# Second layer of a two-layer encoder: values and gates by seven products of halves, with tokens on partitions

## The chip, the cores and the metric

One core of a Trainium2 chip runs the kernel. The metric is the device time of one launch in microseconds (us), taken as the median of several runs. A profile is one further execution, recorded instruction by instruction. The engines are PE (TensorE, the matrix products), DVE (VectorE), ACT (ScalarE), POOL (GpSimd) and SP (SyncE, which here only issues transfers).

## What is computed

The input is `x` of 512 tokens by 1024 channels in float32. Layer 0 mixes latent attention with a pooling mixer. Layer 1, the one that changes, is a bidirectional retention with 4 heads (256 channels for queries and keys, 512 for values). A final RMSNorm follows. Cut to layer 1:

```python
def retention_layer(x, ...):
    h = rms_norm(x, norm_g)
    q, k, v, gate = split(h @ w_in)          # w_in 1024 x 6144: q 1024, k 1024, v 2048, gate 2048
    q, k = rope(q), rope(k) * 256 ** -0.5
    o = forward + backward chunkwise retention(q, k, v)   # equals ((q k^T) * decay matrix) v
    o = (o - mean(o)) * rsqrt(var(o) + 1e-6)              # per head, over its 512 channels
    y = o * gn_g * silu(gate)
    return y @ w_out                         # w_out 2048 x 1024
```

The result is `rms_norm(x + layer 1)`.

## The kernel before

Every product is made in three matmuls (`mm3`, L72, L75, L76): each operand is cut into a rounded half H and the rest L, and H·H, H·L and L·H are added in one PSUM bank. Each matmul has a 128x128 stationary operand and 512 moving columns. A weight tile of 128 x 1024 is loaded by SP into a slot `raw` (3 slots), cast by ACT into `wH` (L108, 4 slots), and DVE subtracts to get `wL` (L109, 3 slots). A weight tile feeds 24 matmuls.

The code is written for one instruction after another, but a list scheduler orders each engine's queue: it takes the work in program order as priority and moves later work ahead where its operands and slots are free by its own cost model. Each engine then runs its queue strictly in that order; a waiting instruction holds all behind it. PSUM has 4 banks `mm`, 2 `sc` and 2 `tr`.

Layer 1 begins in `close_layer` (L651 to L657), which adds the last product of layer 0 to the residual `xT` (channels on partitions), scales it by the norm's gain and splits it into the 8 pairs `h2H`, `h2L`. The norm's factor per token is not multiplied in: it comes from `token_sums` (squares, then two matmuls with ones, L181 and L182), is spread by `bcast` (two matmuls, L209 and L210) into `R`, and multiplies what comes out. `acc_in` transposes the residual to tokens on partitions (L676).

For each head the loop at L828 runs: q and k (`qk_gemm`, 4 column tiles of 24 matmuls), `rope_pair`, the output projection of the head before (`r_out`, 96 matmuls), the decay matrix (`decay`), values (`r_values`, 4 weight tiles, 96 matmuls, tokens on partitions), scores (`r_scores`, 24 matmuls), gates (`r_gates`, 4 weight tiles, 96 matmuls, channels on partitions) and `r_head_out` (48 matmuls, channels on partitions). The group norm's factor needs a sum over channels, so each head has its `token_sums`; with those of the input norm that is five calls, and one `bcast`. After the last head come the projections of heads 2 and 3, and `finish` and `scale_out` make the last norm.

Of the kernel before, what the change touches and what calls it, by code (L numbers as in the profile page):

```python
# [19 lines left out]
P = 128  # L20
# [17 lines left out]
def trunk(ctx: ExitStack, tc: tile.TileContext, x, positions, a_norm_g, a_w_in, a_q_norm_g, a_w_uq,  # L38
# [84 lines left out]
    lg = C("lg", (P, 8))  # L123
    nlb = C("nlb", (P, 8))
    fsum = C("fsum", (P, 16))
    C("fill", (P, 40))
# [518 lines left out]

    h2H, h2L = [None] * 8, [None] * 8
    sqs = S("l1")
# [8 lines left out]
    w_out_quarter(3, ys2, close_layer)  # L658

    def decay(h):  # L660
        e = gp.rearrange("p a b -> p (a b)")[:, :E]
# [2 lines left out]
        act(e, e, AF.Exp)  # L664
        return [e[:, (3 - j) * P:(3 - j) * P + T] for j in range(4)]


    wr = r_w_in[0]
    wo = r_w_out[0]
    acc = [[None] * 2 for _ in range(4)]  # L670

    def acc_in(hf):
# [12 lines left out]
    def qk_gemm(c0, n=2):  # L685
        pts = []
        gemm_T(wr, c0, n, lambda m, pt: pts.append(pt), h2H, h2L)
        return pts

    def rope_pair(pts):  # L690
# [7 lines left out]
        return split(a, "qk"), split(c, "qk")  # L698

    def r_values(h):  # L700
        pts = [PS("mm") for _ in range(4)]
        for kp in range(4):
            uH, uL = wunit(wr[kp * 256:(kp + 1) * 256, 2048 + h * T:2048 + (h + 1) * T]
                           .rearrange("(k p) n -> p k n", p=P), 2, T)
            for k2 in range(2):
                k = kp * 2 + k2
                for t in range(4):
                    tk = slice(t * P, (t + 1) * P)
                    mm3(pts[t], h2H[k][:, tk], h2L[k][:, tk], uH[:, k2], uL[:, k2], k == 0, k == 7)
        vH, vL = [], []  # L710
        for t in range(4):
            v = S("t")
            sm = S("sm", (P, 4))
            act(v, pts[t], AF.Copy, scale=r2[:, t:t + 1], accum_out=sm[:, 0:1])
# [3 lines left out]
            act(hh, v, AF.Identity, bias=sm[:, 1:2])  # L718
            V.scalar_tensor_tensor(out=ll, in0=v, scalar=sm[:, 1:2], in1=f(hh), op0=ALU.add, op1=ALU.subtract)
            vH.append(hh)  # L720
            vL.append(ll)
        return vH, vL

    def r_scores(q, k, ds):
        sH, sL = [], []
        for j in range(4):
            tk = slice(j * P, (j + 1) * P)
            pt = PS("sc")
            for i in range(2):
                mm3(pt, k[i][0][:, tk], k[i][1][:, tk], q[i][0], q[i][1], i == 0, i == 1)  # L730
            s = S("t")
            V.scalar_tensor_tensor(out=s, in0=pt, scalar=0.0625, in1=ds[j], op0=ALU.mult, op1=ALU.mult)
            a, b = split(s, "pt")
            sH.append(a)
            sL.append(b)
        return sH, sL

    def r_gates(h, m0=0, n=4):
        gs = []

        def ev(m, pt):
            t = S("t")
            V.tensor_mul(t, pt, R)  # L743
            g = S("l1")
            act(g, t, AF.Silu)
            gs.append(g)

        gemm_T(wr, 4096 + h * T + m0 * P, n, ev, h2H, h2L)
        return gs

    def r_head_out(h, vv, ss, gs, ytag):
        ys = []
        sq = None
        for m in range(4):
            ms = slice(m * P, (m + 1) * P)
            pt = PS("mm")
            for j in range(4):
                mm3(pt, vv[0][j][:, ms], vv[1][j][:, ms], ss[0][j], ss[1][j], j == 0, j == 3)
            t = S("t")
            act(t, pt, AF.Square)  # L760
            if sq is None:
                sq = t
            else:
                V.tensor_add(sq, sq, t)
            y = S("t")
            V.scalar_tensor_tensor(out=y, in0=pt, scalar=col(GN + h * 4 + m), in1=gs[m], op0=ALU.mult, op1=ALU.mult)
            ys.append(split(y, ytag))
        return ys, sq

    def r_out(h, ys, rs, last=False, mid=None):  # L770
        for hf in range(2):
            us = [wunit(wo[h * T + i * 256:h * T + (i + 1) * 256, hf * T:(hf + 1) * T]
                        .rearrange("(k p) n -> p k n", p=P), 2, T) for i in range(2)]
            for t in range(4):
                tk = slice(t * P, (t + 1) * P)
                n = 2 if last and hf == 1 and t == 3 else 1
                for c in range(n):
                    cs = slice(c * T // n, (c + 1) * T // n)
                    pt = PS("mm")
                    for k in range(4):  # L780
                        mm3(pt[:, :T // n], ys[k][0][:, tk], ys[k][1][:, tk], us[k // 2][0][:, k % 2, cs],
                            us[k // 2][1][:, k % 2, cs], k == 0, k == 3)
# [43 lines left out]

    pend = None
    for h in range(4):  # L828
        if h == 0:
            pts = acc_in(0)  # L830
            pq = qk_gemm(0, 1)
            act(sqs, xT[0], AF.Square)
            for m in range(1, 8):
                t = S("t")
                act(t, xT[m], AF.Square)
                V.tensor_add(sqs, sqs, t)
            acc_set(0, pts)
# [3 lines left out]
            rp = bcast(r2)
            nc.scalar.copy(R, rp)
            V.tensor_mul(cosr, cosr, R)
            V.tensor_mul(sinr, sinr, R)
        else:
            pq = qk_gemm(h * 256)
            pk = qk_gemm(1024 + h * 256, 1)
            pend.append(pow_mhalf(token_sums(psq), 1.0 / T))
        q = rope_pair(pq)
        k = rope_pair(pk + qk_gemm(1024 + h * 256 + P, 1))  # L850
        if h == 0:
            acc_set(1, acc_in(1))
        if pend is not None and h < 3:
            r_out(*pend)
        ds = decay(h)
        if h == 0:
            gs = r_gates(h, 0, 2)
        vv = r_values(h)
        ss = r_scores(q, k, ds)
        gs = gs + r_gates(h, 2, 2) if h == 0 else r_gates(h)  # L860
        ys, sq = r_head_out(h, vv, ss, gs, "y" if h < 3 else "hT")
        if h == 3:
            for i in range(2):
                gt = S("l1")
                nc.scalar.dma_start(gt, final_norm_g[i * T:(i + 1) * T].partition_broadcast(P))
                gF.append(gt)
            own = []
            r_out(*pend, mid=lambda: own.append(pow_mhalf(token_sums(sq), 1.0 / T)))
            r_out(h, ys, own[0], last=True)
# [44 lines left out]
```

## Time and profile before

| | us |
|---|---|
| median of 3 runs | 807.08 (806.32 to 807.74) |
| the profiled execution | 807.98 |
| its span, first to last instruction | 806.2 |
| PE busy in the span | 796.5 (99%), 3590 matmuls |
| DVE busy | 524.1 (65%) |
| ACT busy | 364.4 (45%) |
| POOL busy | 18.9 (2%) |

A busy share counts an engine as busy while any of its instructions is in flight. Matmuls overlap, so one lasts about 390 ns while the next starts 227 ns later; the step from start to start is what a matmul costs.

### The profile page before, as it was taken

How to read it: one execution, taken by the hardware profiler on the slowest of the kernel's cores; microseconds unless marked ns; L12 is line 12 of the kernel's file. 1: busy time of each engine (PE TensorE's matmuls, PEld its weight loads, DVE VectorE, ACT ScalarE, POOL GpSimd, SP SyncE). 2: the span in 40 equal slices, each digit the busy share in tenths (PEclk: the TensorE clock that was granted, in tenths of full speed). 3: DMA queues.
4: the chain of work that ended last, by engine and by line, in shares of the span. 5: the costliest groups of instructions: out<-in, count | busy, mean ns of one | idle time of the engine just before them, and what ended most of it. 6: DMA issues, size and time to landing. Idle time of an engine off the chain costs nothing.

```text
span 806.2 us, 9481 instructions
## 1 busy us (share of the span) xinstructions
PE 796.5 (99%) x3590; PEld 656.1 (81%) x3590; DVE 524.1 (65%) x895; ACT 364.4 (45%) x595; POOL 18.9 (2%) x45
## 2 busy tenths in 40 slices
PE   8999999999999999999999999999999999999996
PEld 6888888888888888888888888888888888888885
DVE  4689976767748687899564648363483535753655
ACT  6645346676627734328254522263232543253222
POOL 0010000000000000000000000000000000000003
PEclk9999999999999999999999999999999999999999
DMA  7523233221222212233323113323123221232112
GB/s 224 150 75 90 85 82 75 54 80 62 72 81 80 79 53 78 79 101 111 103 79 105 52 53 105 98 59 105 53 68 115 79 78 53 85 99 78 53 53 104
DMA packets 93589, 68.30 MB, mean 85 GB/s; under 512 B 7484, under 2 KB 83304, under 8 KB 93544
## 3 DMA queue, kind: packets, MB, share of 16 engines
q1 hardware_dynamic: 93240, 67.18, 28.4%
q8 instruction: 28, 0.46, 0.3%
q10 hardware_dynamic: 304, 0.53, 0.2%
q14 instruction: 17, 0.14, 0.1%
HBM read 64.29 MB, written 2.10 MB: 82 GB/s over the span
## 4 chain that ended last, share of the span: by engine, by line
PE 97%; DMA 1%; POOL 1%; issue 0%; SPq 0%; ACT 0%; DVE 0%; POOLq 0%
PE mm L72 29%; PE mm L75 29%; PE mm L76 29%; PE sc L72 2%; PE sc L76 2%; PE sc L75 2%; PE tr L560 2%; PE sc L541 1%; PE sc L542 1%; DMA l<-in_x_dram 1%; POOL t L820 0%; POOL sm L816 0%; PE tr L182 0%; PE mm L345 0%; PE mm L344 0%
## 5 line engine op out<-in xcount | busy, mean ns | idle before, releaser
L108 ACT CAST wH<-raw 128x1024 fp32r<-128x1024 f32 (+3 forms) x133 | 125.4, 946 | 291.2 <-PE mm L75 137.4
L109 DVE TENSOR_TENSOR wL<-raw,wH 128x1024 fp32r<-128x1024 f32 (+3 forms) x133 | 144.5, 1090 | 94.5 <-PE mm L76 42.1
L72 PE MATMUL mm<-hT,wH 128*128 128x512 f32 x480 | 187.9, 391 | 0.0
L75 PE MATMUL mm<-hT,wH 128*128 128x512 f32 x480 | 187.6, 391 | 0.0
L76 PE MATMUL mm<-hT,wL 128*128 128x512 f32 x480 | 187.6, 391 | 0.0
L76 PEld LDWEIGHTS mm<-hT,wL 128*128 128x128 f32 x480 | 90.6, 189 | 18.9
L75 PEld LDWEIGHTS mm<-hT,wH 128*128 128x128 f32 x480 | 90.4, 188 | 18.7
L72 PEld LDWEIGHTS mm<-hT,wH 128*128 128x128 f32 x480 | 90.5, 189 | 18.5
L75 PE MATMUL mm<-wL,hT 128*128 128x512 f32 (+1 forms) x164 | 63.0, 384 | 0.0
L72 PE MATMUL mm<-wH,hT 128*128 128x512 f32 (+1 forms) x164 | 62.9, 384 | 0.0
L76 PE MATMUL mm<-wH,hT 128*128 128x512 f32 (+1 forms) x164 | 62.8, 384 | 0.0
L786 DVE SCALAR_TENSOR_TENSOR xT<-mm,sm,xT 128x512 f32<-128x512 f32 (+1 forms) x33 | 24.2, 732 | 23.8 <-PE mm L76 23.8
L743 DVE TENSOR_TENSOR t<-mm,R 128x512 f32<-128x512 f32 x16 | 11.1, 691 | 43.2 <-PE mm L76 43.2
L75 PE MATMUL mm<-pt,V 128*128 128x512 f32 x96 | 37.8, 393 | 0.0
L72 PE MATMUL mm<-pt,V 128*128 128x512 f32 x96 | 37.5, 391 | 0.0
L76 PE MATMUL mm<-pt,V 128*128 128x512 f32 x96 | 37.5, 390 | 0.0
L75 PE MATMUL mm<-wL,y 128*128 128x512 f32 x96 | 37.4, 389 | 0.0
L72 PE MATMUL mm<-wH,y 128*128 128x512 f32 x96 | 37.4, 389 | 0.0
L76 PE MATMUL mm<-wH,y 128*128 128x512 f32 x96 | 37.3, 389 | 0.0
L75 PE MATMUL mm<-y,wH 128*128 128x512 f32 x96 | 37.2, 389 | 0.0
L76 PE MATMUL mm<-y,wL 128*128 128x512 f32 x96 | 37.2, 389 | 0.0
L72 PE MATMUL mm<-y,wH 128*128 128x512 f32 x96 | 37.2, 390 | 0.0
(238 smaller groups left out, 1329.8 us busy)
## 6 DMA issues: line engine op xcount, KB each, us to landing
raw<-in_r_w_in_dram SPq DMA_DIRECT2D x48, 512.0 KB, 3.8
raw<-in_a_w_in_dram SPq DMA_DIRECT2D x25, 512.0 KB, 3.9
raw<-in_a_w_out_dram SPq DMA_DIRECT2D x16, 512.0 KB, 3.5
raw<-in_r_w_out_dram SPq DMA_DIRECT2D x16, 512.0 KB, 3.4
l<-in_x_dram SPq DMA_DIRECT2D x8, 256.0 KB, 5.6
out_dram<-t SPq DMA_DIRECT2D x8, 256.0 KB, 2.0
raw<-in_a_w_in_dram SPq DMA_DIRECT2D x4, 384.0 KB, 4.1
raw<-in_a_w_uq_dram SPq DMA_DIRECT2D x8, 192.0 KB, 2.4
```

The source lines that it names most:

```text
L72: i = mm(pt, lhsT=lH, rhs=rH, start=st, stop=False)
L75: mm(pt, lhsT=lH, rhs=rL, start=False, stop=False)
L76: mm(pt, lhsT=lL, rhs=rH, start=False, stop=sp)
L108: then(nc.scalar.copy(h[:, c], raw[:, c]))
L109: then(V.tensor_sub(l[:, c], raw[:, c], f(h[:, c])))
L541: mm(pt, lhsT=st[:, tk], rhs=KH, start=False, stop=False)
L542: mm(pt, lhsT=st[:, tk], rhs=KL, start=False, stop=True)
L560: nc.tensor.transpose(pt[:, t * P:(t + 1) * P], es[t][:, j * P:(j + 1) * P], ident)
L743: V.tensor_mul(t, pt, R)
L786: V.scalar_tensor_tensor(out=a, in0=pt[:, :T // n], scalar=rs[:, t:t + 1], in1=a, op0=ALU.mult, op1=ALU.add)
```

## The change

1. Values and gates of a head are the two halves of a 1024-column block of `w_in`, the tokens are two halves of 256 (`H2`), and the input channels are taken as even and odd blocks of 128. That makes a 2x2 by 2x2 block product, which the new function `vg` computes with seven block products where eight are usual. Each takes 24 matmuls and two weight tiles of its own. Values and gates both come out with tokens on partitions.
2. The seven products need sums of blocks of the activations (`sums_of_halves`, once, in head 0) and sums of blocks of the weights: for two of them (`tt` at its start, and `t3`) a second transfer adds into the landed tile (`G.dma_start(..., accum_op=ALU.add)`, four per head, issued by POOL); for the others DVE adds.
3. `r_head_out` makes outputs with tokens on partitions: the group norm's sum is then an ACT accumulation and `token_sums` goes away; the gated output is transposed on PE (16 transposes of 128x128 per head). The gain `gn_g` moves into the output weights (`out_weights`).
4. The input norm's sums are ACT accumulations on the residual with tokens on partitions (`residual`), and its factor is a per-partition scale (`r2`, `nr2`, `r2s`).
5. Scores are made before `vg`; `r_out` of head 2 runs in head 3's turn. `raw` has 4 slots instead of 3; `tw` (2 slots) holds weight sums.

```diff
@@ close_layer
-        h2H[m], h2L[m] = h, l
+        hH[m], hL[m] = h, l
+        for i, name in enumerate((("A11", "A21"), ("A12", "A22"))[m % 2]):
+            forms[m // 2][name] = (h[:, i * H2:(i + 1) * H2], l[:, i * H2:(i + 1) * H2])
+    def sums_of_halves(i):
+        e, o = S("t"), S("t")
+        for z, m in ((e, 2 * i), (o, 2 * i + 1)):
+            act(z, xT[m], AF.Copy, scale=col(RN + m))
+        z3, z4 = S("t"), S("t")
...
+        V.tensor_sub(z3[:, one], o[:, two], e[:, two])
+        V.tensor_sub(z4[:, one], e[:, one], e[:, two])
...
+            nc.scalar.copy(h, z)
+            V.tensor_sub(l, z, f(h))
...
@@ vg, in place of r_values and r_gates
+        tags = dict(X=("mm", "mm"), Z=("mm", "tr"), Y=("mm", "sc"))
...
+        def load(tag, first, *more):
+            raw = S(tag, (P, 1024))
+            v = raw.rearrange("p (a b) -> p a b", a=2)
+            nc.sync.dma_start(v, first)
+            for one in more:
+                G.dma_start(v, one, accum_op=ALU.add)
+            return raw
+        def product(name, a, ws, first):
+            for i in range(2):
+                wh, wl = S("wH", (P, 1024), F32R), S("wL", (P, 1024), F32R)
+                nc.scalar.copy(wh, ws[i])
+                V.tensor_sub(wl, ws[i], f(wh))
+                for p in range(2):
+                    for k2 in range(2):
...
+        b11 = [load("raw", src(0, 0, i)) for i in rng]
+        tt = [load("tw", src(0, 0, i), src(0, 1, i)) for i in rng]
+        product("A11", "X", b11, True)
+        p1 = [S("t") for _ in rng]
+        for p in rng:
+            nc.scalar.copy(p1[p], ps_["X"][p])
+        b22 = [load("raw", src(1, 1, i)) for i in rng]
+        product("S1", "Z", tt, True)
+        v = [S("t") for _ in rng]
+        for p in rng:
+            V.tensor_add(v[p], ps_["Z"][p], p1[p])
+        t3 = [load("raw", src(0, 1, i), src(1, 1, i)) for i in rng]
+        for i in rng:
+            V.tensor_add(tt[i], tt[i], b22[i])
+        product("S4", "Z", b22, False)
+        b21 = [load("raw", src(1, 0, i)) for i in rng]
+        product("S2", "Y", tt, True)
+        u2 = [S("t") for _ in rng]
+        for p in rng:
+            V.tensor_add(u2[p], ps_["Y"][p], p1[p])
+            V.tensor_add(u2[p], ps_["Z"][p], u2[p])
+            value(p, u2[p])
+        for i in rng:
+            V.tensor_add(tt[i], tt[i], b21[i])
+        product("S3", "Y", t3, False)
+        for p in rng:
+            V.tensor_add(v[p], ps_["Y"][p], v[p])
+            value(2 + p, v[p])
+        product("A12", "X", b21, False)
+        for p in rng:
+            gs[p] = S("l1")
+            act(gs[p], ps_["X"][p], AF.Silu, scale=r2[:, p:p + 1])
+        product("A22", "Y", tt, False)
+        for p in rng:
+            c = S("l1")
+            V.tensor_add(c, ps_["Y"][p], p1[p])
+            act(c, c, AF.Silu, scale=r2[:, 2 + p:3 + p])
...
@@ r_head_out
+        def turn(t):
+            pt = PS("tr")
+            for m in range(4):
+                nc.tensor.transpose(pt[:, m * P:(m + 1) * P], gs[t][:, m * P:(m + 1) * P], ident)
+            ys.append(split(pt, tag))
+        for t in range(4):
...
+            V.tensor_mul(gs[t], pt, gs[t])
+            act(S("t"), pt, AF.Square, scale=r2[:, t:t + 1], accum_out=sq[:, t:t + 1])
+            if t:
+                turn(t - 1)
@@ out_weights, in r_out
+            act(wh[:, c], raw[:, c], AF.Copy, scale=g)
+            V.scalar_tensor_tensor(out=wl[:, c], in0=raw[:, c], scalar=g, in1=f(wh[:, c]), ...)
@@ the loop over heads
+            r_out(h - 1, pend[0], rs)
+        ss = r_scores(q, k, decay(h), B)
+        vv, gs = vg(h)
+        pend = r_head_out(ss, vv, gs, A)
```

## Rows read from the trace of the kernel before

**Rows 1.** The page: busy time of each engine, and the granted clock in 40 slices.

```profile
PE 796.5 (99%) x3590; PEld 656.1 (81%) x3590; DVE 524.1 (65%) x895; ACT 364.4 (45%) x595; POOL 18.9 (2%) x45
PEclk9999999999999999999999999999999999999999
```

**Rows 2.** The page: the chain that ended last, by engine.

```profile
PE 97%; DMA 1%; POOL 1%; issue 0%; SPq 0%; ACT 0%; DVE 0%; POOLq 0%
```

**Rows 3.** Busy time by stage: PE, PEld, DVE, ACT, POOL; granted clock, DMA share, GB/s.

```profile
379.00:404.00 25.00, 25.00 (x123) 21.04 (x122) 15.27 (x34) 10.13 (x17) 1.02 (x1) 1.00 0.32 93
484.50:588.45 103.95, 103.95 (x460) 85.81 (x459) 55.85 (x84) 37.65 (x52) 1.00 (x2) 1.00 0.28 82
```

**Rows 4.** Instructions of PE in order of time, head 1: start, duration.

```profile
481.41 0.39 PE L181 MATMUL tr<-t,ones 128*128 128x512 f32 x1
481.64 0.39 PE L182 MATMUL tr<-t,ones 128*128 128x512 f32 x1
481.87 0.39 PE L72 MATMUL mm<-hT,wH 128*128 128x512 f32 x1
```

**Rows 5.** Groups of PE from 380 us on: busy, mean ns, idle before.

```profile
L181 PE MATMUL tr<-t,ones 128*128 128x512 f32 x5 | 1.9, 389 | 0.0
L209 PE MATMUL tr<-t,ones 128*128 128x512 f32 x1 | 0.4, 389 | 0.0
```

**Rows 6.** The chain in order of time: the transposes of layer 0.

```profile
139.69 0.87 PE tr L560 x8
...
143.07 0.44 PE tr L560 x4
```

**Rows 7.** Groups of DVE and ACT in one head, 484.5 to 588.45 us.

```profile
L109 DVE TENSOR_TENSOR wL<-raw,wH 128x1024 fp32r<-128x1024 f32 x16 | 19.6, 1223 | 23.8 <-PE mm L76 10.5 <-PE mm L75 9.5 <-issue 3.7
L786 DVE SCALAR_TENSOR_TENSOR xT<-mm,sm,xT 128x512 f32<-128x512 f32 x8 | 6.0, 748 | 4.9 <-PE mm L76 4.9
...
L743 DVE TENSOR_TENSOR t<-mm,R 128x512 f32<-128x512 f32 x4 | 2.8, 692 | 11.3 <-PE mm L76 11.3
...
L187 DVE SCALAR_TENSOR_TENSOR t<-tr,ident 128x128 f32<-128x128 f32 x4 | 0.9, 285 | 0.0
...
L662 DVE TENSOR_SCALAR gp<-l,nlb 128x896 f32<-128x896 int16 x1 | 0.7, 679 | 0.0
...
L108 ACT CAST wH<-raw 128x1024 fp32r<-128x1024 f32 x16 | 16.8, 1053 | 47.4 <-PE mm L76 24.8 <-PE mm L75 17.0 <-issue 3.9
L718 ACT ACTIVATE V<-t,sm 128x512 fp32r<-128x512 f32 x4 | 2.9, 724 | 0.0
```

**Rows 8.** Waits over the whole span: us in total, times, longest us.

```profile
ACT wH L108 <- PE mm L75: 137.4, 52, 5.0
...
DVE wL L109 <- PE mm L76: 42.1, 14, 4.3
```

**Rows 9.** Waits of SP's own queue: us in total, times, longest us.

```profile
SPq L100 <- DVE wL L109: 644.5, 110, 19.8
```

**Rows 10.** DMA issues: KB each, median us from issue to landing.

```profile
raw<-in_r_w_in_dram SPq DMA_DIRECT2D x48, 512.0 KB, 3.8
...
l<-in_x_dram SPq DMA_DIRECT2D x8, 256.0 KB, 5.6
```

**Rows 11.** Timeline of POOL: the input norm's and group norm's power.

```profile
484.50 1.01 POOL L174 TENSOR_TENSOR sm<-sm,mhalf 128x4 f32<-128x4 f32 x1 [89.23 <-DVE sm L172]
```

**Rows 12.** Busy time by stage at the start of the program; columns as in rows 3.

```profile
4.50:12.50 8.00, 6.31 (x26) 5.14 (x26) 5.27 (x10) 7.44 (x17) 0.00 (x0) 0.81 1.05 341
```

**Rows 13.** PE in order of time in that stretch, start and duration.

```profile
7.76 0.44 PE L261 MATMUL sc<-ident,l 128*128 128x128 f32 x2 [1.47 <-DMA l<-in_x_dram]
...
9.76 0.63 PE L72 MATMUL mm<-hT,wH 128*128 128x512 f32 x1
10.19 0.63 PE L75 MATMUL mm<-hT,wH 128*128 128x512 f32 x1
...
12.75 0.43 PE L72 MATMUL mm<-hT,wH 128*128 128x512 f32 x1
```

More of the change, by code (lines that the diff above doesn't have):

```diff
@@ L125, in trunk @@
     fsum = C("fsum", (P, 16))
-    C("fill", (P, 40))
+    r2, nr2, r2s = [C(n, (P, 8))[:, 0:4] for n in ("r2", "nr2", "r2s")]
+    C("fill", (P, 16))
     w_in = a_w_in[0]
@@ L644, in trunk @@
     G.tensor_copy(idx, idi)
-    h2H, h2L = [None] * 8, [None] * 8
-    sqs = S("l1")
+    H2 = T // 2
+    forms = [dict() for _ in range(4)]
+    hH, hL = [None] * 8, [None] * 8
     def close_layer(m, pt):
@@ L656, in close_layer @@
         V.scalar_tensor_tensor(out=l, in0=xT[m], scalar=col(RN + m), in1=f(h), op0=ALU.mult, op1=ALU.subtract)
-        h2H[m], h2L[m] = h, l
+        hH[m], hL[m] = h, l
+        for i, name in enumerate((("A11", "A21"), ("A12", "A22"))[m % 2]):
+            forms[m // 2][name] = (h[:, i * H2:(i + 1) * H2], l[:, i * H2:(i + 1) * H2])
     w_out_quarter(3, ys2, close_layer)
+    def sums_of_halves(i):
[3 more added lines that the diff above has]
+        z3, z4 = S("t"), S("t")
+        one, two = slice(0, H2), slice(H2, T)
+        V.tensor_sub(z3[:, one], o[:, two], e[:, two])
+        V.tensor_sub(z4[:, one], e[:, one], e[:, two])
+        V.scalar_tensor_tensor(out=z3[:, two], in0=z3[:, one], scalar=-1.0, in1=e[:, one],
+                               op0=ALU.mult, op1=ALU.subtract)
+        V.scalar_tensor_tensor(out=z4[:, two], in0=o[:, one], scalar=-1.0, in1=z3[:, two],
+                               op0=ALU.mult, op1=ALU.subtract)
+        spare = ["l1"] * 6 + ["x2"] * 2
+        for z, names in ((z3, ("S1", "S2")), (z4, ("S3", "S4"))):
+            hl = []
+            for j in range(2):
+                tag = "pt" if z is z3 else spare[2 * i + j]
+                hl.append(S(tag, dt=F32R))
+            h, l = hl
+            nc.scalar.copy(h, z)
+            V.tensor_sub(l, z, f(h))
+            for j, name in enumerate(names):
+                forms[i][name] = (h[:, j * H2:(j + 1) * H2], l[:, j * H2:(j + 1) * H2])
     def decay(h):
@@ L668, in trunk, with residual @@
     wr = r_w_in[0]
+    wv = wr.rearrange("(i two p) n -> p two i n", two=2, p=P)
     wo = r_w_out[0]
     acc = [[None] * 2 for _ in range(4)]
-    def acc_in(hf):
+    ss2 = S("sm", (P, 8))
+    def residual(hf):
         pts = [PS(tag) for tag in ("tr", "tr", "sc", "sc")]
@@ L697, in rope_pair @@
         V.tensor_add(c, c, d)
[L698 to L712, printed above, removed]
+        return split(a, tag), split(c, tag)
@@ new lines, in vg, with src, value @@
+    def vg(h):
+        tags = dict(X=("mm", "mm"), Z=("mm", "tr"), Y=("mm", "sc"))
+        ps_ = {n: [PS(t) for t in tt] for n, tt in tags.items()}
+        def src(r, c, i):
+            c0 = 4096 - c * 2048 + h * T
+            return wv[:, r, 2 * i:2 * i + 2, c0:c0 + T]
+        def load(tag, first, *more):
[10 more added lines that the diff above has]
+                V.tensor_sub(wl, ws[i], f(wh))
+                last = i == 1
+                for p in range(2):
+                    o = ps_[a][p]
+                    for k2 in range(2):
+                        c = slice(k2 * T, (k2 + 1) * T)
+                        lh, ll = (x[:, p * P:(p + 1) * P] for x in forms[2 * i + k2][name])
+                        mm(o, lhsT=lh, rhs=wh[:, c], start=first and i == 0 and k2 == 0, stop=False,
+                           skip_group_check=True)
+                        mm(o, lhsT=lh, rhs=wl[:, c], start=False, stop=False, skip_group_check=True)
+                        mm(o, lhsT=ll, rhs=wh[:, c], start=False, stop=last and k2 == 1, skip_group_check=True)
+        vv = [None] * 4
+        gs = [None] * 4
+        def value(t, src):
@@ L717, in r_values, with r_scores @@
             ll = S("V", dt=F32R)
[L718 to L725, printed above, removed]
+            act(hh, src, AF.Identity, bias=sm[:, 1:2])
+            V.scalar_tensor_tensor(out=ll, in0=src, scalar=sm[:, 1:2], in1=f(hh), op0=ALU.add, op1=ALU.subtract)
+            vv[t] = (hh, ll)
+        rng = range(2)
+        b11 = [load("raw", src(0, 0, i)) for i in rng]
[35 more added lines that the diff above has]
+            act(c, c, AF.Silu, scale=r2[:, 2 + p:3 + p])
+            gs[2 + p] = c
+        return vv, gs
+    def r_scores(q, k, ds, tag):
+        ss = []
         for j in range(4):
@@ L731, in r_scores @@
             s = S("t")
[L732 to L749, printed above, removed]
@@ L751, in r_head_out @@
-    def r_head_out(h, vv, ss, gs, ytag):
-        ys = []
-        sq = None
-        for m in range(4):
-            ms = slice(m * P, (m + 1) * P)
+            V.scalar_tensor_tensor(out=s, in0=pt, scalar=r2s[:, j:j + 1], in1=ds[j], op0=ALU.mult, op1=ALU.mult)
+            ss.append(split(s, tag))
+        return ss
+    def r_head_out(ss, vv, gs, tag):
+        ys = []
+        sq = S("sm", (P, 4))
+        def turn(t):
[4 more added lines that the diff above has]
+        for t in range(4):
+            tk = slice(t * P, (t + 1) * P)
@@ L768, in r_head_out, with out_scale, out_weights @@
-        return ys, sq
+                mm3(pt, ss[j][0][:, tk], ss[j][1][:, tk], vv[j][0], vv[j][1], j == 0, j == 3)
+            V.tensor_mul(gs[t], pt, gs[t])
+            act(S("t"), pt, AF.Square, scale=r2[:, t:t + 1], accum_out=sq[:, t:t + 1])
+            if t:
+                turn(t - 1)
+        return ys, sq, lambda: turn(3)
+    def out_scale(sq):
+        rs = pow_mhalf(sq, 1.0 / T)
+        V.tensor_mul(rs, rs, r2)
+        return rs
+    def out_weights(h, i, hf):
+        raw = wload(wo[h * T + i * 256:h * T + (i + 1) * 256, hf * T:(hf + 1) * T]
+                    .rearrange("(k p) n -> p k n", p=P), 2, T)[0]
+        wh, wl = S("wH", (P, 1024), F32R), S("wL", (P, 1024), F32R)
+        for k in range(2):
+            g = col(GN + h * 4 + i * 2 + k)
+            c = slice(k * T, (k + 1) * T)
+            act(wh[:, c], raw[:, c], AF.Copy, scale=g)
+            V.scalar_tensor_tensor(out=wl[:, c], in0=raw[:, c], scalar=g, in1=f(wh[:, c]),
+                                   op0=ALU.mult, op1=ALU.subtract)
+        return wh, wl
@@ L770, in r_out @@
     def r_out(h, ys, rs, last=False, mid=None):
         for hf in range(2):
-            us = [wunit(wo[h * T + i * 256:h * T + (i + 1) * 256, hf * T:(hf + 1) * T]
-                        .rearrange("(k p) n -> p k n", p=P), 2, T) for i in range(2)]
+            us = [out_weights(h, i, hf) for i in range(2)]
             for t in range(4):
-                tk = slice(t * P, (t + 1) * P)
                 n = 2 if last and hf == 1 and t == 3 else 1
@@ L828, in trunk @@
     for h in range(4):
+        A, B = ("qk", "y") if h % 2 == 0 else ("y", "qk")
         if h == 0:
-            pts = acc_in(0)
+            res = [residual(0), residual(1)]
+            next(res[0])
             pq = qk_gemm(0, 1)
[L832 to L837, printed above, removed]
+            sums_of_halves(0)
+            sums_of_halves(1)
+            next(res[0])
@@ L838, in trunk @@
             pq += qk_gemm(P, 1)
-            r2 = pow_mhalf(token_sums(sqs), 1.0 / DM)
             pk = qk_gemm(1024, 1)
[L841 to L844, printed above, removed]
+            sums_of_halves(2)
+            sums_of_halves(3)
+            next(res[1])
+            next(res[1])
+            V.tensor_add(ss2[:, 0:4], ss2[:, 0:4], ss2[:, 4:8])
+            V.tensor_copy(r2, pow_mhalf(ss2[:, 0:4], 1.0 / DM))
@@ L845, in trunk @@
+            V.tensor_scalar(out=nr2, in0=r2, scalar1=-1.0, scalar2=1.0, op0=ALU.mult, op1=ALU.mult)
+            V.tensor_scalar(out=r2s, in0=r2, scalar1=0.0625, scalar2=1.0, op0=ALU.mult, op1=ALU.mult)
         else:
-            pq = qk_gemm(h * 256)
+            pq = qk_gemm(h * 256, then=pend[2])
             pk = qk_gemm(1024 + h * 256, 1)
[L848 to L869, printed above, removed]
@@ L870, in trunk @@
-        pend, psq = [h, ys], sq
+            rs = out_scale(pend[1])
+        q = rope_pair(pq, A)
+        k = rope_pair(pk + qk_gemm(1024 + h * 256 + P, 1), A)
+        if pend is not None:
+            r_out(h - 1, pend[0], rs)
+        ss = r_scores(q, k, decay(h), B)
+        vv, gs = vg(h)
+        pend = r_head_out(ss, vv, gs, A)
+    for i in range(2):
+        gt = S("y" if A == "qk" else "qk")
+        nc.scalar.dma_start(gt, final_norm_g[i * T:(i + 1) * T].partition_broadcast(P))
+        gF.append(gt)
@@ L873 @@
+    rs = out_scale(pend[1])
+    r_out(3, pend[0], rs, last=True, mid=pend[2])
 _INS = ['x', 'positions', 'a_norm_g', 'a_w_in', 'a_q_norm_g', 'a_w_uq', 'a_kv_norm_g', 'a_w_ukv',
```

37 lines of the change are left out of this document (17 added, 20 removed).

## The prediction

> **What bounds the kernel now.** I read the page first: PE is busy 99% of the span at the full granted clock, DVE 65%, ACT 45% [rows 1]. Busy time alone proves little for matmuls that overlap, so the chain comes next: 97% of it lies on PE [rows 2], and the reader is to see that no other engine has a share worth naming. Then the stages of layer 1: in a whole head PE is busy for all of 103.95 us, DVE for 55.85 and ACT for 37.65 [rows 3]. Last, the timeline gives the price of a matmul: starts 0.23 us apart [rows 4], and 103.95 us over the 458 matmuls that the code gives a head (456 and two of `token_sums`) is 0.227 us. There are no holes to close: only fewer PE instructions, or new holes, move the time.
>
> **The change on PE.** Per head, values and gates were 8 weight tiles of 24 matmuls, 192; seven products of 24 are 168. That removes 24 in each of four heads: 96 x 0.227 = 21.8 us. `token_sums` goes: five pairs, and the pair of `bcast` [rows 5], 12 x 0.227 = 2.7 us. They sit in PE's stream without a gap [rows 4], so all of that comes off. Added are 16 transposes per head in groups of four. Layer 0 does such groups: on the chain four take 0.44 us and eight 0.87 [rows 6]. 16 groups x 0.44 = 7.0 us; as little as 0.36 a group (5.8 us) if the slower start of the next matmul were counted elsewhere. The residual's 32 transposes only move. q and k, scores, head outputs and projections keep their counts: the operands swap sides, but all stay 128 by 128 against 512 columns. Sum on PE: -21.8 - 2.7 + 7.0 = -17.5 us.
>
> **What must stay hidden: DVE and ACT.** A weight tile now feeds 12 matmuls in `vg` instead of 24. Splits rise from 8 to 14 per head: six more at 1.22 us on DVE and 1.05 on ACT [rows 7]. DVE also gets four 1024-wide adds (4.9 us, taken at the split's 1.22) and ten 512-wide ones on PSUM (6.9 us at 0.69, as L743 [rows 7]). It loses the four gate multiplications (2.8), the sums of `token_sums` (about 2) and the adds of squares (about 2); the output weights cost 1.1 more, as two halves at 0.75 for one at 1.22. DVE goes from 55.85 to about 69 us of a head of 99.7 us. Densest is `vg`: 14 x 1.22 + 4.9 + 6.9 + 3.6 for the centred values = 32.5 us, against 168 x 0.227 = 38.1 us on PE. ACT has 26 us there (14 casts, 8 value passes near 0.7, copies, Silu and its table). Both fit, but they must fit in order. Three `wL` slots let the split of tile n+3 begin when tile n is used up; it is due 5.45 us later and takes 1.22, so a queue may be 4.2 us late. Before, DVE waited for PE for up to 4.3 us at such a split, ACT 5.0 [rows 8]: splits wait for PE, not PE for them.
>
> **New waits in PE's queue.** Banks are written twice. S4 adds into Z after DVE has read S1's result, S3 into Y after the reads of S2's. Each half of a bank pair is complete 6 matmuls (1.36 us) before the product ends, and an add takes 0.69. So if DVE is free it is just in time; if a 1.22 us split is in its way, PE stands up to about 1.2 us, and everything behind it in its queue with it. Two such places with two halves, four heads: 16 waits, of which the first half of each pair is covered best; bounds 0 and 8 x 1.2 = 9.8 us for the other eight. Laying out DVE's work of one `vg` against PE by these durations I find one late add of a few tenths per head, and take 0.8 in all. A22 into Y has A12's 5.45 us as cover, A12 into X four products.
>
> **Head 0.** From 379 to 404 us DVE is busy 15.27 of 25 and ACT 10.13 [rows 3]. `sums_of_halves` adds 3.1 us on DVE and 2.5 on ACT, four times, part of it before 379; ACT also squares the residual (8 x 0.8), while DVE loses sums, broadcast and the scaling of the tables (about 5). That is some 23 of 25 on DVE and 26 to 27 on ACT. An overflow falls where scores would wait for q and k, but A11 needs neither, only two banks that q's rotation frees. Bounds 0 and 5 us; I take 1.0.
>
> **Transfers.** `t3` has the least time. Its slots come free when the first tiles of `vg` are split, about A11's start; its first use is S3, four products or 21.8 us later. A load lands 3.8 us after its issue [rows 10]; cast and split need 2.3. That leaves 15.7 us for an accumulate, which no row shows. From below it is a plain load, 3.8 us; from above I double the slowest landing for reading both operands, 2 x 5.6 = 11.2 us [rows 10]. I take a value nearer the load, since the bytes are those of that row, say 6 us; either way the cost is 0, hidden by A11 to S2. `tt` is loaded a whole `r_out` and more ahead. SP's queue already waits on slots nearly all the time, 110 times for a split [rows 9], with one slot fewer. POOL's queue has little behind the accumulates but the one power per head (1.01 us [rows 11]), and its result is first needed after the rotation.
>
> The only DVE operation of any length in a head that works on one SBUF input is the 0.68 us L662 [rows 7]; the splits and adds have two. The Trainium skill (SBUF — State Buffer, Who interferes with whom) speaks against accumulates issued by POOL: their descriptors go through a port that a DVE copy or tensor_scalar in a two-port mode holds for its whole length, while tensor_tensor does not. By that rule an accumulate would land up to about 0.7 us later, well inside the slack, and the sum would stay; no run here shows one. The Trainium skill (DMA: Bandwidth & Descriptors, Anatomy of one DMA) gives 2.0 us plus bytes over 436 GB/s for a transfer from POOL, 3.2 us for 512 KB, which it does not state for accumulating; by it too the sum stays.
>
> **The sum.** The profiled execution took 807.98 us, 1.8 of them outside its span and none touched by the change; it is 0.9 above the median. -17.5 + 0.8 + 1.0 = -15.7; from the median, 807.08 - 15.7 = 791.4, or about 791 us.
>
> **Rivals.**
> *DVE's order becomes the bound in `vg`.* The queue is fixed by a cost model; where it puts an add that waits for PE ahead of a due split, PE stands at that product's start. For: DVE at 85% there. Against: DVE is at 65% over the span and 54% in a head of layer 1 [rows 1, 3], so above 65% in layer 0, and there too the chain stayed on PE. Price: one late split of 1.2 to 2 us at two or three of the seven products, about 3 us a head, 12 us: 802.
> *Head 0 overflows.* ACT's 27 us in 25 plus a blocked rotation cost 5 us: 795 to 796.
> *Accumulates come late, slower than before.* If an accumulate into `t3` lands beyond 15.7 us, PE idles at S3 in each head, and its clock may fall. At the start of the program PE waited 1.47 us for a load, the granted clock of that stretch was 0.81, a mix of 2.4 GHz and 1.2, and matmuls started 0.43 apart until 12.75 us [rows 12, 13]; about ten of them lost 2 us. With 4 x (wait + 2) above 17.5 the kernel is slower: from 2.4 us of wait, an accumulate of 18 us, five plain loads. At 22 us it costs 4 x 8.3 = 33 us: 823. Against: twice the slowest landing is 11.2.
> *The products are not fewer.* The code has seven calls of `product` with 24 matmuls each, so this is out.
>
> **How the numbers follow.** Forecast 0.58 (own range 789 to 794), DVE's order 0.20, head 0 alone 0.10, late accumulates 0.12. The fastest that the bounds allow is 807.08 - 18.7 = 788.4. The range goes to 803 to take in DVE's order, leaves the late accumulates out, and starts at 787.5 for the scatter of the runs. A measurement of this kernel tells 0.2% (1.6 us) from no change: faster 0.86, same 0.02, slower 0.12, for some of the late accumulates' cases end near 807 and a few of DVE's beyond it.
>
> **What would show it.** Matmuls in heads 1 and 2 again 0.227 us apart and a head of about 99.7 us; 16 transposes per head at 0.44 per four; no L181 or L209 from 380 us on; DVE near 69 us of a head; accumulates of 512 KB on a queue of POOL landing within 12 us. Wrong, if PE's waits name DVE's adds for more than 1 us a head (first rival), ACT's copies around q and k of head 0 (second), or the accumulates (third); wrong in a term, if a transpose group costs other than 0.44.

## The result and the profile after

The changed kernel takes 809.39 us (808.28 to 810.19) where the kernel before takes 807.41 (806.32 to 808.94) in the same comparison: a ratio of 1.0023, 95% interval 1.0012 to 1.0034. It is slightly slower. The forecast of 791 and its range, 787.5 to 803, missed it. The profiled execution took 809.37 us, 1.8 of them outside its span of 807.6; before, the span was 806.2.

The page of the changed kernel, its busy times, granted clock and chain, which answer to [rows 1, 2]:

```profile
PE 784.9 (97%) x3546; PEld 644.5 (80%) x3546; DVE 578.7 (72%) x935; ACT 403.7 (50%) x671; POOL 39.0 (5%) x61
...
PE   8699999999999999999979999999999999999996
...
PEclk9899999999999999999998999999999999999999
...
PE 91%; DVE 2%; DMA 2%; issue 2%; ACT 1%; POOL 1%; SPq 0%; POOLq 0%; DVEq 0%; ACTq 0%
```

PE's work did shrink: 784.9 us busy for 796.5. But its share fell to 97% and the chain now spends 9% of the span off PE, for 3% before. Counted from 0, slice 1 (20 to 40 us) and slice 20 (404 to 424) of PE's row fell, and in the clock's row, full before, slices 1 and 21. Nearly all the lost time is there. Busy time of PE, PEld, DVE, ACT and POOL, granted clock, DMA share and GB/s, in four stretches (columns as in [rows 3]), of the changed kernel:

```profile
29.00:36.00 7.00, 0.91 (x3) 0.47 (x3) 2.87 (x9) 1.37 (x5) 2.56 (x6) 0.75 0.65 119
36.00:42.00 6.00, 6.00 (x21) 4.87 (x21) 4.07 (x6) 1.38 (x2) 0.00 (x0) 0.73 1.04 282
...
416.00:430.00 14.00, 8.77 (x28) 6.34 (x27) 10.91 (x18) 4.26 (x6) 2.03 (x2) 0.76 0.26 39
480.36:580.26 99.90, 99.90 (x450) 82.58 (x449) 69.27 (x92) 46.47 (x67) 5.94 (x6) 1.00 0.44 116
```

The last line is a whole head of layer 1, as [rows 3] has one: 99.90 us where it was 103.95, PE without a hole, DVE 69.27 us. That is what was predicted (99.7 and 69). The others are what was not: PE stands for 6.1 of 7 us at 29 us in layer 0, works at a clock of 0.73 behind it, and stands again for 5.2 of 14 us at the start of layer 1.

**The first hole** lies in layer 0, where the change edits only buffers (a fourth slot of `raw`, another tile for `posf`). The chain of waits of the changed kernel there, start and length, and further down two groups of transposes that answer to [rows 6]:

```profile
22.17 1.39 POOL tw L758
23.57 7.19 issue
30.78 1.24 POOL tw L758
32.02 1.09 POOL sm L175
...
35.45 0.76 PE tr L210
...
147.81 0.87 PE tr L561 x8
...
471.92 0.44 PE tr L852 x4
```

`tw` is the tile of `tt`, the summed weights of layer 1's head 0, first read some 380 us later (ACT's cast at 405.3 us). The planner has put its two loads and its two accumulates at the start of the program, as soon as a slot is there. On POOL the accumulates (the transfers that add) stand ahead of the power of layer 0's input norm (its inverse square root, one small operation on 128x4 numbers). POOL issues the first at 22.17 us, then stands 7.2 us over the second with nothing that the profile shows ("issue"), and only then does the power. POOL and then DVE, changed kernel, in order of time:

```profile
22.17 1.39 POOL L758 DMA_DIRECT2D tw<-in_r_w_in_dram  x1 [20.17 <-DMA tw<-in_r_w_in_dram]
30.78 1.24 POOL L758 DMA_DIRECT2D tw<-in_r_w_in_dram  x1 [7.21 <-issue]
31.54 1.56 POOL L175 TENSOR_TENSOR sm<-sm,mhalf 128x4 f32<-128x4 f32 x1
...
406.83 1.25 POOL L758 DMA_DIRECT2D raw<-in_r_w_in_dram  x1 [66.43 <-DVE wL L765]
415.73 1.22 POOL L758 DMA_DIRECT2D raw<-in_r_w_in_dram  x1 [7.65 <-issue]
416.49 1.53 POOL L175 TENSOR_TENSOR sm<-sm,mhalf 128x4 f32<-128x4 f32 x1
```

```profile
25.80 0.17 DVE L173 TENSOR_SCALAR sm<-sm 128x4 f32<-128x4 f32 x1
33.13 0.17 DVE L199 CAST sm<-sm 128x4 fp32r<-128x4 f32 x1 [7.17 <-POOL sm L175]
...
412.20 0.16 DVE L173 TENSOR_SCALAR sm<-sm 128x4 f32<-128x4 f32 x1
...
418.06 0.17 DVE L958 COPY r<-sm 128x4 f32<-128x4 f32 x1 [5.11 <-POOL sm L175]
418.14 0.69 DVE L740 TENSOR_TENSOR t<-t,t 128x512 f32<-128x512 f32 x1
```

The power's input is ready at 25.97 us and its result is there at 33.1. PE's broadcast of it, L210, comes at 35.45 us behind an idle PE, and the next matmuls start 0.43 apart, as in [rows 13]. PE of the changed kernel in order of time, both holes:

```profile
29.11 0.25 PE L301 MATMUL tr<-ident,t 36*128 36x36 f32 x1
35.45 0.76 PE L210 MATMUL tr<-t,ones 128*128 128x512 f32 x1 [6.09 <-DVE t L206]
...
36.55 0.63 PE L72 MATMUL mm<-hT,wH 128*128 128x512 f32 x1
36.98 0.63 PE L75 MATMUL mm<-hT,wH 128*128 128x512 f32 x1
...
417.73 0.39 PE L775 MATMUL mm<-wH,hT 128*128 128x512 f32 x1
421.51 0.69 PE L772 MATMUL mm<-wH,pt 128*128 128x512 f32 x1 [3.39 <-DVE t L737]
...
424.46 0.80 PE L72 MATMUL sc<-qk,qk 128*128 128x512 f32 x1 [1.83 <-ACT qk L81]
...
438.28 0.50 PE L772 MATMUL tr<-wH,l 128*128 128x512 f32 x1 [0.58 <-DVE t L801]
439.41 0.50 PE L774 MATMUL mm<-wL,l 128*128 128x512 f32 x1 [0.63 <-DVE wL L765]
```

The same transposes of layer 0 that began at 139.69 us before [rows 6] begin at 147.81: 8.1 us later, and no operation of layer 0 was changed.

**The second hole** is the same thing once more, in head 0 of layer 1. Both `t3` accumulates stand on POOL ahead of r2's power, at 406.83 and 415.73. The power's input is ready at 412.36, its result at 418.0. Here DVE passes the wait on: the copy L958 stands in DVE's queue for 5.11 us, and behind it stand L740, L741 and L736 to L738, the rotation. PE waits for L737, which frees the bank of S1 (421.51), and then for a cast behind the rotation, before scores (424.46). With DVE late, two short waits follow inside `vg`: 0.58 us for L801, the add that must read S1's bank before S4 writes to it, and 0.63 us for a split (438.28 and 439.41).

For the account I add up, over all matmul starts more than 0.24 us apart, what each step has above 0.227 us:

| stretch | before | after |
|---|---|---|
| start to 60 us | 5.4 | 13.3 |
| 60 to 340 | 3.3 | 3.4 |
| 340 to 460 | 0.2 | 10.3 |
| 460 to the end | 0.3 | 1.7 |

So the change paid 7.9 + 0.1 + 10.1 + 1.4 = 19.5 us in PE's steps. Nearly all of the last 1.4 is no wait: behind each of the 16 groups of four transposes one matmul starts 0.32 us after the one ahead of it instead of 0.227, and the prediction has that inside its 0.44 a group. The other 18.1 against the predicted -17.5 of PE's work make +0.6; the span grew by 1.4, so this account closes within a microsecond.

### The profile page after: what moved, and what is told of

It is laid out like the page before. It is cut to its first block, busy times and chain, and to the rows that moved or that the text cites. A ratio compares the mean times of both kernels' runs of the same rounds, so it can differ in the third digit from the quotient of the medians.

```text
span 807.6 us, 9591 instructions
## 1 busy us (share of the span) xinstructions
PE 784.9 (97%) x3546; PEld 644.5 (80%) x3546; DVE 578.7 (72%) x935; ACT 403.7 (50%) x671; POOL 39.0 (5%) x61
## 4 chain that ended last, share of the span: by engine, by line
PE 91%; DVE 2%; DMA 2%; issue 2%; ACT 1%; POOL 1%; SPq 0%; POOLq 0%; DVEq 0%; ACTq 0%
PE mm L72 21%; PE mm L76 21%; PE mm L75 21%; PE mm L774 4%; PE mm L775 4%; PE mm L772 4%; PE sc L72 2%; PE tr L561 2%; PE sc L75 2%; PE sc L76 2%; PE sc L774 1%; PE sc L772 1%; PE sc L775 1%; PE sc L542 1%; PE sc L543 1%
## 5 line engine op out<-in xcount | busy, mean ns | idle before, releaser
L72 PE MATMUL mm<-hT,wH 128*128 128x512 f32 x352 | 139.5, 396 | 0.0
L75 PE MATMUL mm<-hT,wH 128*128 128x512 f32 x352 | 138.1, 392 | 0.0
L76 PE MATMUL mm<-hT,wL 128*128 128x512 f32 x352 | 137.7, 392 | 0.0
L108 ACT CAST wH<-raw 128x1024 fp32r<-128x1024 f32 (+3 forms) x85 | 74.4, 884 | 117.0 <-PE mm L75 93.9
L109 DVE TENSOR_TENSOR wL<-raw,wH 128x1024 fp32r<-128x1024 f32 (+3 forms) x85 | 85.5, 1011 | 12.9 <-issue 4.7
L75 PEld LDWEIGHTS mm<-hT,wH 128*128 128x128 f32 x352 | 66.8, 190 | 13.7
L72 PEld LDWEIGHTS mm<-hT,wH 128*128 128x128 f32 x352 | 67.0, 190 | 13.4
L764 ACT CAST wH<-raw 128x1024 fp32r<-128x1024 f32 x32 | 33.7, 1054 | 47.5 <-PE mm L76 20.2
L765 DVE TENSOR_TENSOR wL<-raw,wH 128x1024 fp32r<-128x1024 f32 x32 | 38.9, 1220 | 10.3 <-issue 7.2
L765 DVE TENSOR_TENSOR wL<-tw,wH 128x1024 fp32r<-128x1024 f32 x24 | 29.3, 1220 | 2.9 <-PE tr L774 1.0
L775 PE MATMUL mm<-wH,hT 128*128 128x512 f32 x80 | 31.1, 389 | 0.0
L774 PE MATMUL mm<-wL,hT 128*128 128x512 f32 x80 | 31.1, 389 | 0.0
L772 PE MATMUL mm<-wH,hT 128*128 128x512 f32 x80 | 31.0, 389 | 0.0
```

The source lines that it names most:

```text
L72: i = mm(pt, lhsT=lH, rhs=rH, start=st, stop=False)
L75: mm(pt, lhsT=lH, rhs=rL, start=False, stop=False)
L76: mm(pt, lhsT=lL, rhs=rH, start=False, stop=sp)
L108: then(nc.scalar.copy(h[:, c], raw[:, c]))
L109: then(V.tensor_sub(l[:, c], raw[:, c], f(h[:, c])))
L764: nc.scalar.copy(wh, ws[i])
```

## The experiments

The main theory was that the loss is the order of POOL's queue: accumulates ahead of small powers that PE waits for. Its rivals: head 0's own order of work on DVE and ACT is too dense (the prediction's second rival), the space for the descriptors of POOL's transfers is what the second accumulate waits for, and the accumulating transfers themselves are too dear. "Before" is 808.04 us for the first four kernels and 807.14 for the rest, each measured beside them.

**Only the first pair moved.** The accumulates of `tt` in head 0 are put behind the power of layer 0's input norm on POOL; nothing else changes.

```diff
-        G.tensor_tensor(out=r, in0=v, in1=mhalf, op=ALU.pow)
+        pows.append(G.tensor_tensor(out=r, in0=v, in1=mhalf, op=ALU.pow))
...
-                G.dma_start(v, one, accum_op=ALU.add)
+                if behind is None:
+                    G.dma_start(v, one, accum_op=ALU.add)
+                else:
+                    with tc.issue_after(behind.ins):
+                        G.dma_start(v, one, accum_op=ALU.add)
...
-        tt = [load("tw", src(0, 0, i), src(0, 1, i)) for i in rng]
+        tt = [load("tw", src(0, 0, i), src(0, 1, i), behind=pows[0] if h == 0 else None) for i in rng]
```

> The two accumulates into tw for head 0 are queued on POOL behind the power of layer 0's input norm instead of ahead of it; their plain loads stay where they were. Theory A (POOL's queue: the power waits behind the second accumulate): the power is done near 27 us instead of 32, PE's idle stretch of 6.3 us at 29 us and the 0.43 us spacing behind it go, the transposes of layer 0 come 8 us earlier (near 139.7), and the time is 8 us under the changed kernel, 800 to 802. Rival B (the 2 MB of early loads take bandwidth from layer 0's weights): the idle stretch stays, under 2 us gained. Head 0 of layer 1 is untouched in both.

Measured: 800.73 us (799.39 to 801.35), ratio 0.9905 (0.9890 to 0.9919). POOL of this kernel in order of time:

```profile
27.12 1.04 POOL L177 TENSOR_TENSOR sm<-sm,mhalf 128x4 f32<-128x4 f32 x1 [25.11 <-DVE sm L175]
28.10 1.40 POOL L764 DMA_DIRECT2D tw<-in_r_w_in_dram  x1
34.51 1.24 POOL L764 DMA_DIRECT2D tw<-in_r_w_in_dram  x1 [5.01 <-issue]
```

The power comes at 27.12 instead of 31.54, PE is busy for all of 29 to 36 us, and the steps' excess before 60 us falls from 13.3 to 5.9. The changed kernel had 1.0023; the difference, 0.0118, is 9.5 us (give or take 1.5 by the two intervals) from the place of two instructions in one queue. By the profiled executions 7.4 us of it are at the start and 1.5 in head 0 (excess 8.8 for 10.3), where the first `t3` accumulate landed 7.3 us after its issue, for 8.6 before; the expectation had head 0 untouched. The second accumulate still stands 5 us over "issue", but now nothing waits behind it.

**Only the second pair moved.** The same with `t3` of head 0, behind r2's power.

```diff
-        t3 = [load("raw", src(0, 1, i), src(1, 1, i)) for i in rng]
+        t3 = [load("raw", src(0, 1, i), src(1, 1, i), behind=r2_pow if h == 0 else None) for i in rng]
```

> The two accumulates into t3 of head 0 are queued on POOL behind the power of layer 1's input norm instead of ahead of it. Theory A: that power follows its sums within 1.5 us instead of 5, DVE's rotation of q comes 4 to 5 us earlier, PE's idle of 3.8 us at S1 shrinks to under 1, and the time is 4 to 7 us under the changed kernel, 802 to 805; the t3 accumulates land later, but S3 is some 10 us off. Rival C (ACT and DVE have too much to do in head 0, whatever POOL does): under 1.5 us gained. The start is untouched in both.

Measured: 804.14 us (803.57 to 804.50), ratio 0.9948 (0.9934 to 0.9963). POOL of this kernel:

```profile
412.74 1.02 POOL L177 TENSOR_TENSOR sm<-sm,mhalf 128x4 f32<-128x4 f32 x1 [72.01 <-DVE sm L175]
413.71 1.25 POOL L764 DMA_DIRECT2D raw<-in_r_w_in_dram  x1
420.46 1.22 POOL L764 DMA_DIRECT2D raw<-in_r_w_in_dram  x1 [5.50 <-ACT qk L81]
```

The stand of 3.4 us before S1 is gone, and the excess from 340 to 460 us falls from 10.3 to 4.5. For the second accumulate the profile names ACT, but here too the first had landed 0.3 us ahead of it (6.4 us after its issue). So 5.8 us of head 0's loss is POOL's queue, and 4.5 us is not. By the ratios, 1.0023 and 0.9948, it is 6.1 us (give or take 1.5).

**Both pairs moved** (the two edits together).

> Both orders of the two runs before in one kernel. Theory A: the gains add, 12 to 15 us under the changed kernel, 794 to 797, faster than the kernel before by over 1%. B and C: 806 to 809.

Measured: 794.83 us (793.11 to 796.02), ratio 0.9839 (0.9822 to 0.9855). The two add up: 9.5 and 6.1 us alone, 14.9 together (give or take 1.6). All three times lie in the ranges of theory A. What is left in head 0, by its stretch in this kernel (columns as above) and DVE there:

```profile
395.00:425.00 30.00, 27.47 (x126) 21.91 (x125) 25.55 (x39) 16.26 (x28) 3.44 (x3) 1.00 0.32 62
```

```profile
401.18 0.16 DVE L963 TENSOR_TENSOR sm<-sm 128x4 f32<-128x4 f32 x1 [3.52 <-ACT t L722]
```

DVE waits 3.5 us in its queue for the last squares of the residual on ACT, r2 comes late once more, and the rotation behind it: PE is short of 2.5 us in this stretch, 1.3 of it before the scores and 1.2 at S4, as in the changed kernel. The changed kernel has the same 3.52 us wait of DVE, at 411.52. That is the prediction's second rival, next to the new one.

**More room for descriptors, order unchanged.** The changed kernel with twice the descriptor scratch for POOL's transfers; the bytes come out of buffers of layer 0's pooling mixer (`WB`), which uses 544 of their columns.

```diff
-    WB = 576
+    WB = 544
...
-dynamic_dma_scratch_size=1024)
+dynamic_dma_scratch_size=2048)
```

> POOL's descriptor space is doubled from 1024 to 2048 bytes per partition (room comes from the pooling buffers, 544 instead of 576 columns, which layer 0 does not use beyond 544); every order is as in the changed kernel. Theory A, with the space as the reason why the second accumulate of a pair stands 7 to 8 us: the pair starts 1.3 to 4 us apart (the second load's landing decides), the first power ends near 27 to 29 us, and the time is 8 to 13 us under the changed kernel, 796 to 801. Rival D (the second waits for its own load, or for the first accumulate's completion for another reason): pairs stay 8 to 9 us apart and the time stays at 809.

Measured: 801.89 us (801.48 to 803.74), ratio 0.9926 (0.9911 to 0.9941). POOL of this kernel, head 0's two pairs and the next `tt`:

```profile
21.87 1.39 POOL L758 DMA_DIRECT2D tw<-in_r_w_in_dram  x1 [19.85 <-DMA tw<-in_r_w_in_dram]
27.27 1.22 POOL L758 DMA_DIRECT2D tw<-in_r_w_in_dram  x1 [4.01 <-DMA tw<-in_r_w_in_dram]
28.04 1.53 POOL L175 TENSOR_TENSOR sm<-sm,mhalf 128x4 f32<-128x4 f32 x1
404.38 1.24 POOL L758 DMA_DIRECT2D raw<-in_r_w_in_dram  x1 [66.26 <-ACT wH L764]
409.29 1.22 POOL L758 DMA_DIRECT2D raw<-in_r_w_in_dram  x1 [3.67 <-DMA raw<-in_r_w_in_dram]
...
454.19 1.24 POOL L758 DMA_DIRECT2D tw<-in_r_w_in_dram  x1 [42.61 <-DVE wL L109]
456.25 1.19 POOL L758 DMA_DIRECT2D tw<-in_r_w_in_dram  x1 [0.81 <-DVE V L787]
```

"issue" is gone: the second of each of head 0's pairs now waits for its own load, and in the later `tt` it follows 2.06 us behind. The landings agree. In the changed kernel the first of head 0's two pairs landed 8.3 and 8.6 us after its issue, at 30.5 and 415.4, and the second was issued 0.3 us behind that (30.78 and 415.73); here the first landed at 29.9 and 411.7, and the second had been issued before, at 27.27 and 409.29. So the unnamed 7 us were space for descriptors, which came free when the first accumulate had landed. The time fell by 7.8 us, just short of the 8 to 13 expected, and the pairs stand 5 us apart for the 1.3 to 4 expected: rival D was right in that the second waits for its own load as well. The excess is 10.4 before 60 us and 4.2 in head 0. In head 0 the room alone was enough; at the start it was not, since there the second accumulate waits for its own load and the power waits with it (PE still stands 3.4 us). Room shortens the wait in front of the power; order removes it.

**Both pairs moved, and head 0 reordered.** To find the 4.5 us that were left, the residual's sums and r2 are formed ahead of the second half of q and the first of k.

```diff
             next(res[0])
-            pq += qk_gemm(P, 1)
-            pk = qk_gemm(1024, 1)
             sums_of_halves(2)
...
             V.tensor_scalar(out=r2s, in0=r2, scalar1=0.0625, scalar2=1.0, op0=ALU.mult, op1=ALU.mult)
+            pq += qk_gemm(P, 1)
+            pk = qk_gemm(1024, 1)
```

> As the run with both powers first; besides, in head 0 the sums of halves, the second half of the residual and the norm's factor stand in the program ahead of the second q tile, not behind the first k tile. Theory E (what is left in head 0 is order: DVE waits 3.5 us for ACT's squares while q could be rotated): that wait goes, PE's excess between 340 and 460 us falls from 4.5 to 1 to 3 us, and the time is 1 to 3.5 us under that run, 791.5 to 794. Rival C (DVE has too much to do around the rotation, whatever the order): within 0.8 us of it.

Measured: 790.99 us (790.80 to 791.10), ratio 0.9799 (0.9786 to 0.9812), the 791 of the forecast. The start of layer 1 in this kernel (columns as above), and r2's power on POOL:

```profile
395.00:425.00 30.00, 30.00 (x133) 24.67 (x132) 27.73 (x42) 13.52 (x19) 3.49 (x3) 1.00 0.46 106
```

```profile
396.30 1.02 POOL L177 TENSOR_TENSOR sm<-sm,mhalf 128x4 f32<-128x4 f32 x1 [64.09 <-DVE sm L175]
```

r2's power runs at 396.30, where the kernel with both pairs moved had its sums only at 401.2; PE has no hole in head 0, and a whole head is 99.90 us again. The excess from 340 to 460 us is 0.4, less than the 1 to 3 expected, and the time is just under the 791.5 to 794; the waits at S4 are gone too. By the ratios this order is worth 3.2 us. No stretch has more than 0.2 us of excess over the kernel before, but for the 1.2 behind the transposes: all of the missing time is accounted for.

**The same with the larger descriptor scratch** (`WB = 544`, 2048).

> The run before it in this call, with POOL's descriptor space doubled as well. Accumulates of a pair come closer together (2 to 5 us), but no power stands behind one any more, so the theory expects no change: within 0.8 us. If the late second accumulates held up S1 or S3 in heads 1 to 3, it would be over 1.5 us faster.

Measured: 792.36 us (791.18 to 793.67), ratio 0.9816 (0.9801 to 0.9831). The first pair is now issued without a stand between its two:

```profile
26.79 2.65 POOL L764 DMA_DIRECT2D tw<-in_r_w_in_dram  x2
```

There is no gain. The median is 1.4 us higher, more than the 0.8 expected, but the interval overlaps that of the kernel without the room. Once nothing that PE needs stands behind the accumulates, their room is worth nothing that these runs can tell.

**No accumulating transfers.** The changed kernel, but SP loads the second tile too and DVE adds it.

```diff
-                G.dma_start(v, one, accum_op=ALU.add)
+                other = S("raw", (P, 1024))
+                nc.sync.dma_start(other.rearrange("p (a b) -> p a b", a=2), one)
+                V.tensor_add(raw, raw, other)
```

> The changed kernel without accumulating transfers: the second tile is loaded into raw by SP, and DVE adds it (four more adds of 1024 columns per head, 4.9 us). POOL then has only its powers. Theory A: the start is as in the kernel before (8 us gained), the wait for the power in head 0 goes as well, and DVE at about 74 of 100 us still hides the adds in heads 1 to 3 (a head of 99.9 to 101 us): 794 to 799. Rival F (the accumulating transfers are needed, since DVE is the bound in vg without them): a head takes over 102.5 us, and the time is 803 or more.

Measured: 797.36 us (797.00 to 798.98), ratio 0.9882 (0.9868 to 0.9896). A whole head of this kernel:

```profile
480.36:580.26 99.90, 99.90 (x449) 82.50 (x448) 73.24 (x97) 46.29 (x68) 1.01 (x1) 1.00 0.37 116
```

A head still takes 99.90 us with 4 us more on DVE, which is hidden. The start is whole again (excess 5.8). Head 0 keeps 6.4, for the order of its residual is unchanged; the next run tests that.

**The same with head 0 reordered.** The last two edits together.

> The run with sums by DVE, in the order of head 0 of the first run of this call. Theories A and E: 1 to 3.5 us under the run with sums by DVE, 792 to 797. Rival C: within 0.8 us of it.

Measured: 790.48 us (788.95 to 791.50), ratio 0.9791 (0.9776 to 0.9807), not to be told from the version with accumulates (its interval 0.9786 to 0.9812 overlaps). It is 6.9 us under the run with sums by DVE, where at most 3.5 were expected and no less than 792: the excess of head 0 falls from 6.4 to 1.3, so the order was worth more here than with accumulates (3.2). Why is not shown beyond that. The accumulating transfers buy nothing here: DVE has the room. As the changed kernel used them, they brought most of the loss: without them it is 11.4 us faster by the ratios, 1.0023 and 0.9882.

## Why the prediction was wrong

**PE's sum was right.** A head of 99.90 us against 99.7 (the prediction's own terms make 99.8); four transposes at 0.44 us on the chain, 0.45 with the late start of the matmul behind them; no hole in heads 1 to 3. The reordered kernel's 790.99 meets the forecast's number, but it is another kernel, and part of that is luck: the 1.8 us that the forecast adds for new waits and for head 0 were not needed in it (about 0.2 in head 0).

**DVE's and ACT's load was right.** DVE is busy 69.27 us of a head against 69; in `vg` of head 1, from 526.77 to 566.21 us, DVE is busy 33.7 and ACT 26.8, where 32.5 and 26 were laid out. The first rival, DVE's order as the bound in `vg`, did not come in heads 1 to 3: from 460 us on PE's steps have 1.7 us of excess for all of them together, 1.4 of that behind transposes, where it asked for 3 a head. So the 0.8 us for new waits between the products is not seen there either. In head 0, where DVE was late from the rotation on, such waits did come, 0.58 and 0.63 us at S4; with r2 early they were gone.

**The price of an accumulate was nearly right.** The page's list of transfers of the changed kernel, KB each and median us from issue to landing:

```profile
raw<-in_r_w_in_dram SPq DMA_DIRECT2D x48, 512.0 KB, 3.7
...
raw<-in_r_w_out_dram SPq DMA_DIRECT2D x16, 512.0 KB, 5.4
tw<-in_r_w_in_dram SPq DMA_DIRECT2D x8, 512.0 KB, 3.6
tw<-in_r_w_in_dram POOLq DMA_DIRECT2D x8, 512.0 KB, 7.1
raw<-in_r_w_in_dram POOLq DMA_DIRECT2D x8, 512.0 KB, 6.2
```

Medians of 6.2 and 7.1 us, where 6 was taken between 3.8 and 11.2; single ones took 5.9 to 8.8. The 3.2 us that the Trainium skill (DMA: Bandwidth & Descriptors, Anatomy of one DMA) gave in the prediction do not hold for an accumulate here. The Trainium skill (Collectives: The Full Stack, The bandwidth ceiling) says of additions made by DMA in collectives that they run at about half the rate of copies, because both operands are read. The ratios here, 6.2 to 3.7 and 7.1 to 3.6, are 1.7 and 2.0, of that size. But POOL's issuing (1.2 to 1.4 us) is in them, POOL issued no plain transfer to compare with, and plain loads of `w_out` beside the accumulates had a median of 5.4 us; so no run here shows the reason.

**The step that failed is "Transfers".** It costed the accumulates by their landing and at 0, and said that "`tt` is loaded a whole `r_out` and more ahead" and that "POOL's queue has little behind the accumulates but the one power per head". Three things were wrong in it:

- *Place.* Head 0's `tt` needs nothing but a slot, so the planner issued it at the start of the program, in layer 0, where the prediction did not look at POOL's queue. The power that stood behind it there is layer 0's. Price: 9.5 us (first experiment), 7.4 of it seen at the start.
- *Who waits.* The power's result "is first needed after the rotation" by its data, but DVE's copy of r2 stands in DVE's queue ahead of the rotation, so a late power stops the rotation and PE. Price: 6.1 us (second experiment).
- *What it costs to issue.* Only landing was bounded. Issuing takes POOL 1.2 to 1.4 us. Before that POOL stands until the plain load into the same tile has landed and, for the second of a pair, until there is room: 8.6 us between the first two (22.17 to 30.78), 8.9 between the second two (406.83 to 415.73). The Trainium skill (DMA: Bandwidth & Descriptors, Anatomy of one DMA) says that a transfer's semaphore waits are made by the engine that issues it, before dispatch; POOL's stand of 4.01 us for the load of `tw`, in the run with more room, agrees. A small instruction behind it on POOL pays for it.

The rival "accumulates come late, slower than before" had the sign and the engine but not the way. It let the *data* come late at S3, four times, from an accumulate of 18 us on; no matmul waited for one. What came late was the next instruction of POOL's queue, twice, with accumulates of 5.9 to 8.8 us. Its remark on the clock held: after the holes the granted clock of the stretch was 0.73 to 0.76, a mix of 2.4 GHz and 1.2, and matmuls started 0.43 us apart.

The rival "head 0 overflows" (5 us, chance 0.10, as an alternative to the forecast) was true as well, beside the failed step: 4.5 us remained with both pairs moved, and forming r2 ahead of the second half of q took all but 0.4 away. The prediction gave that step 1.0 us. It added up ACT's load over the stretch, but not that the last squares come last in ACT's order and r2 waits for them.

## What to carry to other kernels

When a change issues a transfer from an engine that also computes, read what stands behind the issue in that engine's queue, at each place where the planner may put it, and not only where the code has it: an operation whose input is ready early can be put at the start of the program. Cost the issue (its wait for an operand, for a slot and for room) apart from the landing. A tiny operation on a lightly used engine (POOL was busy 2% of the span before) can lie one step from the path: at the start 5.6 us of delay there cost 7.9 in PE's steps, 1.9 of them in matmuls that started slowly behind the idle stretch.

## What the runs showed of the hardware

- In the changed kernel an accumulating transfer of 512 KB from POOL landed 5.9 to 8.8 us after its issue (medians 6.2 and 7.1); plain ones of 512 KB from SP had medians of 3.4 to 5.4 us by tensor.
- With 1024 as descriptor scratch the second accumulate of a pair was issued 6.4 to 8.9 us after the first, with a stand of 5.0 to 7.7 us that the profile calls "issue", and 0.3 us after the first had landed; with 2048 it followed without a stand, two issues in 2.65 us, where its load and slot were ready.
- After 6.1 us of idle PE (up to 35.45) two matmuls started 0.55 us apart and the next 0.43, until 39.11; from 39.43 on it was 0.23 again. The granted clock of 36 to 42 us was 0.73, a mix of 2.4 GHz and 1.2. The nine steps from 35.45 to 39.43 took 3.98 us, for 2.04 at 0.227 each.
